# Merge of a hybrid diffusion block: branch sums for 1024 tokens at a time, then the output product as seven half-size products

## The chip, the cores and the metric

The kernel runs on one core of a Trainium2 chip. The metric is device time in microseconds (us), the median of the timed runs. The core has five engines with an instruction queue each: PE multiplies matrices into eight PSUM banks, DVE, ACT and POOL do elementwise work (POOL never reads PSUM), and SP issues nearly all transfers. All data is float32. For a product, each operand is split into a rounded part "hi" (type fp32r) and the remainder "lo", and three matmuls hi x hi, hi x lo, lo x hi are added up.

## The reference, cut to what matters

```python
# per token: attn_x (512), gm_x (512), ga_x, gb_x (1024 each); SEQ = 2048, D = 1024
y = sigmoid(ga_x) * (attn_x @ w_br_attn) + sigmoid(gb_x) * (gm_x @ w_br_gm)
x = x + g1 * (y @ w_out)
h2 = rmsnorm(x, norm2_g) * (1 + sc2) + sh2
x = x + g2 * (square(relu(h2 @ w_ff1)) @ w_ff2)      # D_FF = 4096
```

The whole layer also makes the modulation vectors, one combined input projection, the gMLP gating and grouped-query attention over 256 context and 2048 latent keys. They come before the part that changes.

## The kernel before, in words

The work is in four stages that PE goes through in order: projection, attention (`attend`), `merge`, and the feed-forward part (`ffn`). Tokens come in four blocks of 512 (`TB`), b = 0 to 3; spilled tensors in memory carry intermediate results between stages.

**Merge.** For each block b there are two steps. The branch step runs m = 0 to 7 over 128 output channels each: `fetch` loads the two 512x128 slices of the branch weights (`br_raw`, L853), splits them into hi and lo (`br_weights`, helper `split`: hi by ACT on L138, lo by POOL or DVE on L142) and loads two gate tiles (`gate_in`, L868), always two m ahead. 24 matmuls (L170 to L172, helper `mm3`) make two sums in PSUM; DVE multiplies each by its gate (L903), adds them (L906), and `split` makes the hi and lo of y. The outer step then multiplies y (eight tiles of 128 channels x 512 tokens) with `w_out`, which `load_w_out` has split once in block 0: four token tiles x two column halves x 24 matmuls. DVE multiplies by g1 (L941), adds x (L942), SP stores x1 (L944), and ACT sums the squares (L947) for the next norm. The inputs of the next block's branch step (`br_inputs`: attention and gMLP rows, softmax denominators, split into hi and lo, L832 to L842) are made beside the outer step.

**Feed-forward.** It works on two blocks of 1024 tokens, `blk` = 0 and 1, and computes each product of 2x2 half-size blocks with seven half-size products in place of eight (Strassen's scheme in Winograd's form). `h_ops` (L964 to L1010) reads x1, scales it by the norm (DVE, L981: one 128x2048 instruction for each of four kk), transposes it on PE (L176, 16 for each kk), applies scale and shift (ACT, L990), and makes the seven token operands with four DVE sums (L998 to L1007) and seven hi/lo pairs (`halves`: ACT on L961, DVE on L962). For block 0 this is called after the merge, with nothing beside it; for block 1 it is a side generator of the second product of block 0, `ff2`. `w1_ops` makes the weight operands of a group of 256 hidden channels (load L1017, DVE L1024 to L1046, ACT L1032 to L1045), one group ahead of its use. `ff1_group` (L1076 to L1078, helper `product`) does seven products of 12 matmuls. `w2_ops` prepares `w_ff2` in seven operands and stores them.

`ff2` has 7 x 8 steps of 24 matmuls, each on a chunk of two operands that `ff2_chunk` loads from memory (two transfers of 512 KB, L1162), rounds (ACT, L1163) and subtracts (DVE, L1164). A chunk takes four tiles of 4 KB per partition of the tag `f4`, which has 12 slots, so three chunks fit; the chunk of step n+2 is asked for in step n. The seven products go in the order 0, 1, 5, 6, 4, 2, 3. Products 0, 1, 5, 6, 3 add up in one set of four banks, 4 and 2 in another. After product 0, ACT copies the banks out (L1203); after 1, DVE makes a quarter of the output (L1176, two instructions a token tile) and ACT restores the banks from the copy (L1206); after 5 and 6 ACT copies again.

**Order.** A compile-time scheduler places the instructions of each queue by estimated times; `order` at the end adds constraints: tiles of one tag take their slots in program order, and SP's instructions inside `ff2` keep program order. At run time each queue is strictly in order. SBUF is given out in pools: `join` for the merge and `back` for the feed-forward part cannot be open together.

Of the kernel before, what the change touches and what calls it, by code (L numbers as in the profile page):

```python
# [9 lines left out]
F32 = mybir.dt.float32  # L10
# [8 lines left out]
P = 128  # L19
# [24 lines left out]
NCH = NG // 2  # L44


def f32(ap):
# [7 lines left out]
    "join": {"gt": 6, "bw": 14, "y": 16, "wo": 18, "xt": 3, "jk": 4},  # L55
    "back": {"h": 56, "f8": 3, "f4": 12, "f2": 16, "fs": 5},
# [7 lines left out]
class Kern:  # L64
# [50 lines left out]
    def small(self, shape, dtype=F32):  # L115
        return self.sb("fs" if "back" in self.open_pools else "ts", shape, dtype)
# [61 lines left out]
    def constants(self):  # L178
# [17 lines left out]
        self.ss2 = cp.tile([P, SEQ // P], F32, name="ss2")  # L196
# [16 lines left out]
        def operands(n):  # L213
            return [
                [
                    dp.tile([2, P, TB], F32, tag=f"{n}{p}_{c}", name=f"{n}_d{p}_{c}")
                    for c in range(NCH)
                ]
                for p in range(7)
            ]  # L220

        self.ao_d = [operands(f"ao{blk}") for blk in range(2)]
        self.wo_d = operands("w2o")
# [589 lines left out]
    def load_w_out(self):  # L813
        nc = self.nc
        self.wo = []
        self.g1b = self.sb("g1", [D])
        nc.sync.dma_start(self.g1b, self.g1_d.partition_broadcast(P)[:, 0, :])
        for k in range(KC):
            st = self.sb("wo", [D])
            nc.sync.dma_start(st, self.I["w_out"][0, k * P : (k + 1) * P, :])  # L820
            h, l = self.sb("wo", [D], F32R), self.sb("wo", [D], F32R)
            self.split(st, h, l, lo_eng="dve")
            self.wo.append((h, l))
            yield

    def br_inputs(self, b, out):
        nc = self.nc
        for nm, src in (("g", self.gm_d[b]), ("a", self.at_d[b])):
            out[nm] = []
            for k in range(4):  # L830
# [12 lines left out]
                h, l = self.sb("in", [TB], F32R), self.sb("in", [TB], F32R)  # L843
# [4 lines left out]
    def br_raw(self, m):  # L848
        out = {}
        for nm, key in (("a", "w_br_attn"), ("g", "w_br_gm")):  # L850
            out[nm] = self.sb("bw", [4, P])
            src = self.I[key][0][:, m * P : (m + 1) * P]
            self.nc.sync.dma_start(out[nm], src.rearrange("(k p) c -> p k c", p=P))  # L853
        return out

    def br_weights(self, raw, lo_eng="pool"):
        ws = {}
        for nm in ("g", "a"):
            wh, wl = self.sb("bw", [4, P], F32R), self.sb("bw", [4, P], F32R)
            self.split(raw[nm], wh, wl, lo_eng=lo_eng)  # L860
            ws[nm] = (wh, wl)
        return ws
# [8 lines left out]

    def merge(self, first, start, last):
        nc = self.nc
        for _ in start:
            pass
        self.close("mid", "base")
        self.open("join")
        steps = [(b, m) for b in range(NB) for m in range(KC)]
        it = iter(steps)
        q = []  # L880
        w_out = self.load_w_out()

        def fetch(lo_eng="pool"):
            s = next(it, None)
            if s is not None:
                q.append((self.br_weights(self.br_raw(s[1]), lo_eng), self.gate_in(*s)))

        inp = first
        early = [(s, self.br_raw(s[1])) for s in (next(it), next(it))]
        for s, raw in early:  # L890
            q.append((self.br_weights(raw, "dve"), self.gate_in(*s)))
        for b in range(NB):
            y = []
            for m in range(KC):
                fetch("pool" if b else "dve")
                ws, gt = q.pop(0)
                for nm in ("g", "a"):
                    ps = self.bank([TB])
                    wh, wl = ws[nm]
                    for k in range(4):  # L900
                        h, l = inp[nm][k]
# [674 lines left out]
```

## Time and profile before

| what | value |
|---|---|
| median of 3 timed runs | 3160.06 us (3157.05 to 3162.28) |
| profiled execution, first to last instruction (its span) | 3152.1 us |
| median less that span | 8.0 us |
| mean granted PE clock in that execution | 0.989 |
| merge in it, first branch matmul to last outer matmul | 1478.42 to 1847.40 us after the start |
| last matmul of the kernel issued | 3146.58 us |

The profile shows one execution, and gives no time for it besides its span. A row of the timeline gives the start, the duration, the engine, the line, the operation, the tiles (written <- read) and, in brackets, how long the engine had stood idle and what ended that. A matmul's duration is that of the pipeline; how fast PE works is read from the starts of neighbours. Rows of a stretch give the busy time of every engine (x instructions), the granted PE clock (1 is full) and the DMA engines' share and rate. "In", "bw", "gt", "y", "wo", "f", "h", "ac" are tags of tiles, "b" is PSUM.

### The profile page before, as it was taken

How to read it: one execution, taken by the hardware profiler on the slowest of the kernel's cores; microseconds unless marked ns; L12 is line 12 of the kernel's file. 1: busy time of each engine (PE TensorE's matmuls, PEld its weight loads, DVE VectorE, ACT ScalarE, POOL GpSimd, SP SyncE). 2: the span in 40 equal slices, each digit the busy share in tenths (PEclk: the TensorE clock that was granted, in tenths of full speed). 3: DMA queues.
4: the chain of work that ended last, by engine and by line, in shares of the span. 5: the costliest groups of instructions: out<-in, count | busy, mean ns of one | idle time of the engine just before them, and what ended most of it. 6: DMA issues, size and time to landing. Idle time of an engine off the chain costs nothing.

```text
span 3152.1 us, 38056 instructions
## 1 busy us (share of the span) xinstructions
PE 3057.4 (97%) x13892; PEld 2308.7 (73%) x13892; DVE 1944.7 (62%) x2797; ACT 1352.2 (43%) x2058; POOL 919.3 (29%) x634
## 2 busy tenths in 40 slices
PE   7999999999999999999999969999999999999999
PEld 4888788877655555555877858888777888888777
DVE  4735666566666677767644369777664576654445
ACT  3353434333454545454322135444543344443433
POOL 1423324241688888887134300000000000000000
PEclk9999999999999999999999989999999999999999
DMA  6353555535100000003754347988575644445665
GB/s 200 111 180 117 199 158 172 190 108 166 41 14 4 21 8 18 11 8 121 242 179 161 117 137 275 312 307 291 196 251 204 224 144 148 158 152 191 209 214 200
DMA packets 332174, 485.42 MB, mean 154 GB/s; under 512 B 33969, under 2 KB 166321, under 8 KB 331986
## 3 DMA queue, kind: packets, MB, share of 16 engines
q1 hardware_dynamic: 324002, 478.38, 45.4%
q10 hardware_dynamic: 7984, 4.61, 0.5%
q8 instruction: 109, 1.79, 0.2%
q14 instruction: 79, 0.65, 0.1%
HBM read 348.56 MB, written 134.35 MB: 153 GB/s over the span
## 4 chain that ended last, share of the span: by engine, by line
PE 78%; DVE 8%; DMA 5%; POOL 3%; issue 2%; ACT 2%; SPq 0%; ACTq 0%; DVEq 0%; POOLq 0%
PE b L1077 12%; PE b L1078 12%; PE b L1076 11%; PE b L1468 8%; PE b L170 7%; PE b L171 7%; PE b L172 7%; PE b L1435 5%; PE b L1454 4%; PE b L1400 3%; PE b L176 2%; DMA f<-w2o_d 1%; DMA w<-in_w_in 1%; DVE f L1164 1%; DMA bw<-in_w_br_gm 1%
## 5 line engine op out<-in xcount | busy, mean ns | idle before, releaser
L1164 DVE TENSOR_TENSOR f<-f,f 128x1024 fp32r<-128x1024 f32 x224 | 273.2, 1224 | 266.3 <-ACT f L1163 260.8
L1411 DVE TENSOR_REDUCE ts<-b 128x1 f32<-128x512 f32 x512 | 314.8, 683 | 175.7 <-PE b L1400 175.7
L1163 ACT CAST f<-f 128x1024 fp32r<-128x1024 f32 x224 | 235.3, 1053 | 332.4 <-DMA f<-ao_d 291.5
L1078 PE MATMUL b<-h,f 128*128 128x512 f32 x896 | 349.4, 390 | 9.1 <-DVE f L1033 7.2
L1077 PE MATMUL b<-f,f 128*128 128x512 f32 x896 | 351.5, 392 | 4.7 <-DVE f L1164 4.0
L1076 PE MATMUL b<-h,f 128*128 128x512 f32 x896 | 349.5, 391 | 3.4 <-ACT f L1032 3.4
L1078 PE MATMUL b<-f,f 128*128 128x512 f32 x896 | 349.4, 390 | 0.0
L1077 PE MATMUL b<-h,f 128*128 128x512 f32 x896 | 349.4, 390 | 0.0
L1076 PE MATMUL b<-f,f 128*128 128x512 f32 x896 | 307.5, 392 | 12.3 <-ACT f L1163 5.5
L1484 POOL TENSOR_TENSOR ac<-ac,p 128x512 f32<-128x512 f32 x216 | 296.3, 1403 | 71.4 <-ACT p L1458 70.5
L1458 ACT ACTIVATE p<-b 128x512 f32<-128x512 f32 x384 | 199.6, 616 | 157.5 <-PE b L1454 147.6
L142 POOL TENSOR_TENSOR w<-w,w 128x1024 fp32r<-128x1024 f32 x60 | 147.3, 2455 | 402.6 <-ACT w L138 204.1
L1484 POOL TENSOR_TENSOR ac<-ac,t 128x512 f32<-128x512 f32 x160 | 232.1, 1475 | 1.4 <-ACT t L1458 1.4
L138 ACT CAST w<-w 128x1024 fp32r<-128x1024 f32 x120 | 125.8, 1049 | 218.7 <-DMA w<-in_w_in 185.7
L170 PE MATMUL b<-t,w 128*128 128x512 f32 x512 | 204.8, 400 | 5.6 <-DVE t L584 5.2
L1076 PEld LDWEIGHTS b<-f,f 128*128 128x128 f32 x896 | 167.7, 188 | 53.6 <-ACT f L1163 9.6
L1077 PEld LDWEIGHTS b<-f,f 128*128 128x128 f32 x896 | 168.6, 188 | 46.0 <-DVE f L1164 11.6
L1078 PEld LDWEIGHTS b<-h,f 128*128 128x128 f32 x896 | 168.6, 188 | 45.7 <-DVE f L1033 7.9
L171 PE MATMUL b<-t,w 128*128 128x512 f32 x512 | 201.3, 393 | 0.0
L172 PE MATMUL b<-t,w 128*128 128x512 f32 x512 | 201.1, 393 | 0.0
L1435 PE MATMUL b<-t,t 128*128 128x512 f32 x576 | 198.7, 415 | 1.8 <-ACT p L1458 1.6
L1076 PEld LDWEIGHTS b<-h,f 128*128 128x128 f32 x896 | 168.9, 188 | 39.1 <-ACT f L1032 3.8
(217 smaller groups left out, 6137.9 us busy)
## 6 DMA issues: line engine op xcount, KB each, us to landing
w<-in_w_in SPq DMA_DIRECT2D x120, 512.0 KB
ao_d<-f SPq DMA_DIRECT2D x224, 256.0 KB
f<-ao_d SPq DMA_DIRECT2D x112, 512.0 KB
f<-w2o_d SPq DMA_DIRECT2D x112, 512.0 KB
f<-in_w_ff SPq DMA_DIRECT2D x48, 1024.0 KB
w2o_d<-f SPq DMA_DIRECT2D x112, 256.0 KB
md<-in_w_mod SPq DMA_DIRECT2D x32, 512.0 KB
f<-x_d SPq DMA_DIRECT2D x64, 256.0 KB
```

The costliest lines, as they stand in the source:

```text
L170: mm(ps, sh, mh, start=start, stop=False)
L171: mm(ps, sh, ml, start=False, stop=False)
L172: mm(ps, sl, mh, start=False, stop=stop)
L1076: mm(ps, wh, hh, start=start and k == 0, stop=False, skip_group_check=True)
L1077: mm(ps, wh, hl, start=False, stop=False, skip_group_check=True)
L1078: mm(ps, wl, hh, start=False, stop=k == len(w) - 1, skip_group_check=True)
L1163: nc.scalar.copy(h, f32(l))
L1164: nc.vector.tensor_tensor(out=l, in0=f32(l), in1=f32(h), op=ALU.subtract)
L1411: nc.vector.tensor_reduce(out=self.mx[:, t, h, c : c + 1], in_=ps[h], axis=AX.X, op=ALU.max)
L1435: self.nc.tensor.matmul(self.pts[j][h], k.KA[c][self.kv][:, ks], self.qa[h], start=True, stop=False, skip_group_check=True,)
L1468: nc.tensor.matmul(self.o[h * HD : (h + 1) * HD, :], k.V[c][:, i, self.kv * HD : (self.kv + 1) * HD], pt[h], start=j == 0, stop=j == NKT - 1,)
L1484: nc.gpsimd.tensor_tensor(out=self.acc[e][:, h], in0=old[:, h], in1=pt[h], op=ALU.add)
```

## The change

- The merge goes through pairs of blocks. `branches` (new) does the branch step of a block. For the first block of a pair, y is kept in SBUF (tag `y`) and stored as operands 0 and 1; for the second, every two m DVE makes the sums of Winograd's form from the four y tiles (four instructions of 128x512) and SP stores operands 3, 4, 5, 6 and 2. y is no longer split into hi and lo there.
- `w_out` is scaled by g1 (one DVE instruction of 128x2048 for each of four steps), combined with four DVE sums and stored in seven operands by `row_ops` (the renamed body of `w2_ops`), beside the branch step of block 0: a 1 MB load and seven stores of 256 KB for each step, two yields of it for each m.
- `rows` (the renamed body of `ff2`) does the output product as well: `out_rows(blk, side)` calls it with two chunks for each of seven products, so 14 steps of 24 matmuls for 1024 tokens. It loads x (four transfers of 256 KB for each of four quarters), DVE adds it, ACT sums squares into `ss2`, now for each column half, and writes the junk over the source.
- `h_ops(0)` becomes the side generator of `out_rows(1)` with two yields per step. For block 0 its 128x2048 scaling and its four sums go to POOL.
- `br_inputs` of the next block is made beside the branch step, in a second tag `in2` where needed.
- The weights of both branches of an m now share a tile of tag `f4`: three such tiles for an m (raw, hi, lo), one ACT and one POOL instruction of 128x1024. The `flow` tags, `f4` among them, are opened before the merge.
- In `rows`, so in `ff2` too, the order of the products is 0, 1, 5, 6, 3, 4, 2, and the result is written over the residual tile; in `ff2` the product with g2 is written over its source, which for products 1 and 3 is PSUM.

The core of the diff:

```diff
-    "join": {"gt": 6, "bw": 14, "y": 16, "wo": 18, "xt": 3, "jk": 4},
-    "back": {"h": 56, "f8": 3, "f4": 12, "f2": 16, "fs": 5},
+    "flow": {"f8": 3, "f4": 12, "f2": 16, "fs": 5},
+    "join": {"in2": 16, "gt": 6, "y": 8},
+    "back": {"h": 56},
...
+    def br_weights(self, m, lo_eng):
+        raw = self.sb("f4", [2, 4, P])
+        for i, key in enumerate(("w_br_gm", "w_br_attn")):
             src = self.I[key][0][:, m * P : (m + 1) * P]
+            self.nc.sync.dma_start(raw[:, i], src.rearrange("(k p) c -> p k c", p=P))
+        h, l = self.sb("f4", [2, 4, P], F32R), self.sb("f4", [2, 4, P], F32R)
+        self.split(raw, h, l, lo_eng=lo_eng)
+        return h, l
...
+    def branches(self, b, inp, fetch, y0, blk_ops, sides):
...
+        for m in range(KC):
+            fetch()
+            (wh, wl), gt = self.bq.pop(0)
...
+            y = self.sb("f2" if i else "y", [TB])
+            tt(y, gt["a"], gt["g"], add)
+            if i == 0:
+                y0[m] = y
+                nc.sync.dma_start(dst[f], y)
+            else:
+                y1[f] = y
+                if f:
...
+                    for p, src in ((3, a22), (4, s1), (5, s2), (6, s3), (2, s4)):
+                        nc.sync.dma_start(dst[p], src)
+            for it in sides:
+                next(it, None)
...
+            sides = [more]
+            if b == 0:
+                sides = [closing(), more, w_out, w_out]
+            elif b == 1:
+                sides = [w_out, w_out, more]
+            self.branches(b, inp, fetch, y0, self.yo_d[b // 2], sides)
...
+            if b == 1:
+                self.ready = [self.chunk(self.yo_d[0], self.wy_d, 0, 0)]
+                self.out_rows(0, iter(()))
         self.close("join", "pre")
         self.open("back")
+        self.ready = [self.chunk(self.yo_d[1], self.wy_d, 0, 0)]
+        h = [[None] * (KC // 2) for _ in range(7)]
+        self.out_rows(1, self.h_ops(0, h))
+        return h
...
+        def finish(i, j, t, src, x):
+            cs = slice(j * TB, (j + 1) * TB)
+            nc.vector.tensor_tensor(out=x, in0=src, in1=x, op=ALU.add)
+            col = (2 * blk + i) * TT + t
+            nc.scalar.activation(src, x, AF.Square, accum_out=self.ss2[:, j, col : col + 1])
+            return self.x1_d[2 * blk + i][t * P : (t + 1) * P, cs]
+
+        self.rows(self.yo_d[blk], self.wy_d, MCH, source, finish, side, 2)
...
+        eng = nc.vector if blk else nc.gpsimd
...
-            nc.vector.tensor_tensor(out=xv, in0=xv, in1=rb, op=ALU.mult)
+            eng.tensor_tensor(out=xv, in0=xv, in1=rb, op=ALU.mult)
...
-        order = (0, 1, 5, 6, 4, 2, 3)
-        steps = [(p, c) for p in order for c in range(NCH)]
+        order = (0, 1, 5, 6, 3, 4, 2)
+        steps = [(p, c) for p in order for c in range(chunks)]
         banks = {}
         for n, (p, c) in enumerate(steps):
             if n + 2 < len(steps):
-                ready.append(self.ff2_chunk(blk, *steps[n + 2]))
+                ready.append(self.chunk(ao, wo, *steps[n + 2]))
```

More of the change, by code (lines that the diff above doesn't have):

```diff
@@ L811, in attend, with br_inputs @@
         self.fixed.append(range(begin, self.here()))
[L813 to L826, printed above, removed]
+    def br_inputs(self, b, out, tag="in"):
         nc = self.nc
```

264 lines of the change are left out of this document (127 added, 137 removed).

## The prediction

> **What bounds the kernel now.** First the page's head and its slices, to see which engine sets the pace and where it doesn't.
>
> ```profile
> span 3152.1 us, 38056 instructions
> PE   7999999999999999999999969999999999999999
> ```
>
> PE is busy nearly always; each slice is 78.8 us, and the one weak slice, the 24th, is the hand-over from the merge to the feed-forward part. So a change pays in PE instructions saved, in PE's waits, and in that slice. Second, stretches of the merge: branch and outer steps of block 0, of block 1, the outer steps of blocks 2 and 3, the hand-over.
>
> ```profile
> core 0: us, PE busy (x) PEld busy (x) DVE busy (x) ACT busy (x) POOL busy (x), PEclk, DMA share, GB/s
> 1478.00:1526.00 48.00, 47.58 (x195) 37.16 (x196) 33.71 (x47) 21.24 (x34) 9.20 (x6) 0.96 0.83 271
> 1526.00:1570.00 44.00, 43.93 (x195) 36.00 (x193) 24.15 (x33) 12.34 (x20) 5.92 (x4) 1.00 0.72 238
> 1570.00:1615.00 45.00, 45.00 (x194) 36.25 (x193) 17.68 (x23) 11.49 (x20) 24.31 (x18) 1.00 0.48 148
> 1615.00:1664.00 49.00, 46.26 (x194) 36.97 (x193) 21.57 (x29) 11.58 (x20) 8.16 (x6) 0.97 0.55 186
> 1709.00:1759.00 50.00, 45.72 (x191) 36.42 (x190) 21.70 (x29) 11.52 (x20) 8.23 (x6) 0.97 0.48 164
> 1804.00:1848.00 44.00, 43.79 (x194) 35.90 (x192) 11.04 (x17) 4.07 (x7) 1.29 (x1) 1.00 0.13 48
> 1848.00:1894.00 46.00, 18.26 (x78) 14.94 (x79) 41.02 (x77) 27.56 (x45) 0.00 (x0) 0.67 0.64 189
> ```
>
> A step takes about 45 us whatever DVE, ACT and POOL do: PE bounds it. Only block 0's branch step is also near another limit, with DMA at 0.83. Third, the timeline of PE at the end of the merge.
>
> ```profile
> 1834.71 0.39 PE L170 MATMUL b<-wo,y 128*128 128x512 f32 x1
> 1835.39 0.39 PE L170 MATMUL b<-wo,y 128*128 128x512 f32 x1
> 1859.24 6.48 PE L176 MATMUL b<-ident,f 128*128 128x128 f32 x32 [11.45 <-DVE f L981]
> 1871.60 3.61 PE L176 MATMUL b<-ident,f 128*128 128x128 f32 x16 [3.40 <-ACT f L990]
> 1878.63 0.79 PE L1076 MATMUL b<-h,f 128*128 128x512 f32 x1 [3.43 <-ACT f L1032]
> 1887.07 0.80 PE L1078 MATMUL b<-h,f 128*128 128x512 f32 x1 [7.22 <-DVE f L1033]
> 1893.62 0.50 PE L1078 MATMUL b<-h,f 128*128 128x512 f32 x1 [1.92 <-DVE f L1040]
> ```
>
> The duration of 0.39 is not what a matmul costs: the two L170 rows are three matmuls and 0.68 us apart, 0.227 us each. A step of 24 is 5.44 us.
>
> **Fewer matmuls: -21.8 us.** The outer steps have 768; seven products x 2 chunks x 24 x 2 are 672. 96 x 0.227 = 21.8.
>
> **The waits inside the merge: -12.9 us.** The four outer steps take 44 + 49 + 50 + 44 = 187 us by their rows, 768 x 0.227 = 174.1. The difference is the wait for the hi and lo of the last y, which goes with its split:
>
> ```profile
> PE b L170 <- ACT y L138: 3.5, 3, 1.5
> PE b L172 <- POOL y L142: 3.5, 4, 1.0
> ```
>
> The rest of it is half clock after such waits (0.97 in two rows).
>
> **The hand-over: -36.1 us, of which 2 come back.** From 1848 to 1894 there are 46 us with 13 useful matmuls (2.9 us). The 64 transposes remain; at full clock 16 of them take 1.76 us (the chain of waits, in order of time), 7.0 in all:
>
> ```profile
> 2240.89 1.76 PE b L176 x16
> ```
>
> 46 - 2.9 - 7.0 = 36.1. Of these, 7.22 + 3.43 + 1.92 = 12.6 us belong to `w1_ops(0)`, which the change doesn't name. At the end of `ff2(0)` the same preparation is hidden, since the scheduler may issue it ahead; I take 2 us for it, between 0 and 12.6.
>
> **Block 0's transfers: +18 us, blocks 1 to 3: +4.** Sizes are in the DMA view:
>
> ```profile
> bw<-in_w_br_gm SPq DMA_DIRECT2D x32, 256.0 KB
> w2o_d<-f SPq DMA_DIRECT2D x112, 256.0 KB
> ```
>
> In units of 256 KB (0.262 MB), block 0's branch step now moves 16 of weights, 16 of gates, 12 of `br_inputs(1)`, 16 of `w_out`, 28 operand stores of `w_out` and 8 of y: 96 units, 25.2 MB, against 48 us x 271 GB/s = 13.0 MB. The densest long stretch is
>
> ```profile
> 1940.00:2000.00 60.00, 60.00 (x266) 49.70 (x265) 47.46 (x64) 27.24 (x40) 0.00 (x0) 1.00 0.91 318
> ```
>
> 318 / 0.91 = 349 GB/s at full share: 72 us, where PE needs 45. All of it goes through SP's one queue, so the weights for m+2 stand behind stores that wait for DVE. The last stores (2.1 MB, 6 us) aren't needed by PE: 66 us against 48. If the compile order puts the stores off into block 1 the term could be 0; with DVE's stores blocking SP it could be 27. Block 1 has 64 units, 48 us plus the 6 left over, of which the last 12 don't hold PE up: 47 for 45. Blocks 2 and 3 have 52 units each, 39 us under 45: +1 each (0 to 5). DVE in block 0 gets 16 sums and four scalings more (about 20 us by the durations quoted further down) on 34; that stays under 66.
>
> **out_rows(0): +19 us.** A chunk from its issue to the last subtraction, in `ff2`:
>
> ```profile
> 3130.45 0.36 SPq L1162 DMA_DIRECT2D f<-ao_d  x1
> 3130.91 0.42 SPq L1162 DMA_DIRECT2D f<-w2o_d  x1
> 3131.38 1.90 SPq L1185 DMA_DIRECT2D f<-x_d  x4
> ```
>
> ```profile
> 3136.65 1.23 DVE L1164 TENSOR_TENSOR f<-f,f 128x1024 fp32r<-128x1024 f32 x1 [0.27 <-ACT f L1163]
> ```
>
> That is 7.4 us. `ff2` hides it with three chunks in 12 slots of `f4`. Here `fetch` has already put the weights of block 2, m = 0 and 1, into four slots, and nothing frees them until the product is over. Two chunks fit: step n+2's load is issued when step n ends and must be ready when step n+1 ends. A step then takes (7.4 + 5.44) / 2 = 6.4 us; 12 x 1.0 = 12. Behind that waiting load on SP stand the four loads of x. For product 1 they come after its last step; x lands behind the chunk (about 5.5 us), then DVE adds, ACT squares and restores the bank for product 5 (0.7 + 2 x 0.6): 5.5 us more than the ordinary wait, and 1.7 of half clock. 12 + 7 = 19; 0 if the slots come free in time, 35 if the load is slower (second rival).
>
> **out_rows(1): +14 us.** PE needs 14 x 5.44 + 7.0 = 83.2 us. POOL's work beside DVE's:
>
> ```profile
> 1462.11 13.39 DVE L1481 TENSOR_TENSOR ac<-ac,p 128x1024 f32<-128x1024 f32 x6
> ```
>
> ```profile
> 1467.74 8.89 POOL L1484 TENSOR_TENSOR ac<-ac,t 128x512 f32<-128x512 f32 x4
> 1494.25 1.29 POOL L142 TENSOR_TENSOR y<-gt,y 128x512 fp32r<-128x512 f32 x1 [3.21 <-PE b L171]
> ```
>
> ```profile
> L1164 DVE TENSOR_TENSOR f<-f,f 128x1024 fp32r<-128x1024 f32 x224 | 273.2, 1224 | 266.3 <-ACT f L1163 260.8
> L142 POOL TENSOR_TENSOR w<-w,w 128x1024 fp32r<-128x1024 f32 x60 | 147.3, 2455 | 402.6 <-ACT w L138 204.1
> ```
>
> ```profile
> L962 DVE TENSOR_TENSOR h<-f,h 128x512 fp32r<-128x512 f32 x28 | 19.2, 685 | 0.0
> ```
>
> Alone a DVE instruction takes 1.22 and a POOL one 1.29; together each takes 2.22. They take turns, at 2.22 for 2.51. DVE instructions with both inputs in SBUF: 28 subtractions x 1.22, 28 halves and 8 sums of x x 0.685: 59 us. POOL: four scalings at twice 2.455 and 16 sums at 1.29: 40. 99 x 2.22 / 2.51 = 88 us; 16 sums that read PSUM (0.685 each), the norm's small instructions and the order within the queues make it about 97, 14 over PE. Transfers are 104 units, 78 us. Bounds: 0 (POOL's turns fall into gaps) to 30. The Trainium skill, "SBUF — State Buffer", section "Who interferes with whom", says that a DVE instruction with two SBUF inputs and a reading GpSimd instruction exclude each other for the whole instruction. By it the 88 are 99 and the term is 25; the measured pair decides.
>
> **ff2 and the start: +6.5 us.** The last product was 3 (two DVE instructions a tile) and is now 2 (three):
>
> ```profile
> 3143.61 0.69 DVE L1176 TENSOR_TENSOR f<-b,g2b 128x512 f32<-128x512 f32 x1 [5.73 <-PE b L1078]
> 3147.61 1.28 DVE L1176 TENSOR_TENSOR f<-f,f 128x512 f32<-128x512 f32 x2
> ```
>
> Eight end 5.28 us after the first starts, 0.66 each; twelve take 7.9, so the last store leaves 2.6 us later. After product 1 the restore waits for one DVE instruction more (the product with g2 is in PSUM now; a write there shows no price, I take the same 0.685):
>
> ```profile
> PE b L1076 <- ACT b L1206: 4.8, 4, 1.7
> ```
>
> ```profile
> 2247.00:2250.00 3.00, 3.00 (x9) 2.35 (x8) 2.60 (x5) 3.00 (x6) 0.00 (x0) 0.52 0.29 111
> 2295.00:2301.00 6.00, 3.59 (x14) 2.47 (x14) 6.00 (x9) 2.51 (x4) 0.00 (x0) 1.00 1.13 335
> ```
>
> ```profile
> 2245.62 0.50 PE L1076 MATMUL b<-f,f 128*128 128x512 f32 x1 [1.84 <-ACT f L1203]
> ```
>
> A wait of 1.84 us at 2245 was followed by 3 us at clock 0.52; the 1.7 us of L1206, in the stretch from 2295, left it at 1.00. With 0.7 more, those waits in each `ff2` may cross into that: 2 x 0.7 and one half clock in two, and product 3 now waits for the copies after 6: +2.4 (0 to 8). The Trainium skill, "TensorE: Matmul & The Clock Gate", section "What's actually happening", drops the clock only after an idle window of about 3.4 us; by it, waits under that are free of half clock and my sum is some 3 us lower, but the 1.84 us row speaks against it. At the start the weights of both branches must land before one cast of 1024 elements: +1.5 (0 to 6).
>
> **Sum.** -21.8 - 12.9 - 36.1 + 2 + 18 + 4 + 19 + 14 + 6.5 = -7.3 us against the profiled 3152.1, so 3144.8 there. The runs' median lies 8.0 above that span, and 8.0 is added again: 3152.8.
>
> **The rivals.**
>
> *All the cover holds (chance 0.2).* Stores slip into block 1, two chunks suffice, POOL falls into gaps: the terms +18, +19 and +14 shrink to 2, 5 and 3. -7.3 - 41 = -48: 3112. For it: in `ff1(0)` PE never waited at a DMA share of 0.91. Against: 25.2 MB can't go through in 45 us at 349 GB/s.
>
> *Slots of `f4` starve out_rows(0), slower than before (0.3).* A chunk load under dense traffic has taken
>
> ```profile
> 2305.71 10.87 DMA f<-w2o_d
> ```
>
> 10.9 us, and with cast and subtraction 13.1. A step is then (13.1 + 5.44) / 2 = 9.3, 12 steps cost 46 in place of 12: +34, in all +27: 3187. It decides from 6.44 + 7.3 / 12 = 7.0 us a step, a load of 8.7 us; from there the change loses. For it: 88 units in this stage, and product after product with loads of x and stores of x1. Against: the bare load is 7.4.
>
> *The operands are not made in time (0.05).* If POOL and DVE in turn finish `h_ops(0)` only after the last product, up to 15 us of the hand-over come back: 3168.
>
> **How the numbers follow.** The forecast, 3140 to 3165 around 3153, has 0.45. Within 0.2% is 6.3 us, about what a measurement of this kernel tells from no change. Faster by more: all of the first rival (0.2) and half of the forecast (0.23), 0.43. Within: 0.17 of the forecast and 0.05 of the slower cases, 0.22. Slower: the rest, 0.35. The range leaves a tenth out on each side: 3110, the first rival, to 3190, the second.
>
> **What would show it.** Right: 672 matmuls of the output product; no gap over 5 us between the merge and `ff1`; block 0's branch step at 60 us or more with DMA above 0.9; out_rows(0) at 6.4 us a step, PE waiting for the chunk's cast and once for the restore after product 1; out_rows(1) at 95 us or more with DVE instructions lengthened beside POOL; the end 2.6 us longer after the last matmul. Wrong: block 0's step under 55 us, or either product under 85 us (the first rival); a step over 7 us in out_rows(0) (the second).

## The result, and the profile after

The changed kernel takes 3276.74 us (median of four runs, 3273.64 to 3280.43) against 3158.56 for the kernel before in the same series (3153.25 to 3162.28): 1.0375 times as long, 95% interval 1.036 to 1.039. It was forecast at 3152.8, and it is 118 us slower. The profiled execution has a span of 3277.2 us, 125.1 more than before, at a mean granted clock of 0.975.

The stretches of the merge in the profile after, with the columns of the prediction's second fence: the branch steps of blocks 0 and 1; the time from there to the first step of out_rows(0); out_rows(0) with the branch steps of blocks 2 and 3 (the scheduler interleaves the end of one with the start of the next); out_rows(1).

```profile
1479.00:1623.00 144.00, 109.76 (x388) 80.10 (x388) 87.55 (x98) 23.64 (x28) 36.27 (x14) 0.87 0.86 275
1623.00:1645.00 22.00, 0.39 (x3) 0.16 (x1) 11.99 (x15) 6.66 (x9) 4.78 (x2) 0.56 0.78 252
1645.00:1848.00 203.00, 181.05 (x719) 140.08 (x720) 106.75 (x137) 66.31 (x97) 33.98 (x14) 0.94 0.70 228
1848.00:1980.00 132.00, 100.82 (x404) 76.57 (x403) 88.07 (x82) 70.20 (x113) 42.17 (x20) 0.88 0.66 218
```

Before, PE was busy in 0.91 to 1.00 of each step (the prediction's second fence). Here it is busy in 0.76 of blocks 0 and 1 and of out_rows(1), and in next to nothing of the 22 us ahead of out_rows(0). From the first branch matmul to the first matmul of `ff1` 500.9 us pass, against 400.2 before: 100.7 of the 125.1. What PE waited for in the first two stretches (engine, line, what ended the wait; total, times, longest):

```profile
PE b L172 <- ACT f L140: 22.2, 8, 5.4
PE b L1108 <- ACT f L1195: 21.6, 1, 21.6
PE b L174 <- POOL f L144: 14.4, 9, 2.0
```

L140 and L144 are the split of the branch weights: they came late. L1195 is the cast of the first chunk of out_rows(0). And in out_rows(1), where no wait leads:

```profile
PE b L1109 <- DVE f L1196: 9.8, 7, 4.7
PE b L1108 <- ACT f L1195: 9.5, 6, 5.4
PE b L178 <- POOL f L1005: 5.4, 1, 5.4
PE b L1108 <- ACT b L1241: 3.6, 1, 3.6
```

Waits cost more than themselves. At full clock the starts of neighbouring matmuls are at most 0.24 us apart; in the merge after, 182 matmuls follow at 0.30 to 0.45 us (half clock, after a wait), before 37. That alone is 31 us against 6.

The rest of the loss lies behind the merge: `ff1(0)` and `ff1(1)` are 1.9 and 10.5 us longer, though `ff1(0)` lost 8 us of waits and half clock, most at its start; `ff2(0)` is 7.9 longer, `ff2(1)` with the kernel's end 3.5. One row tells most of `ff1`, the same 270 us within `ff1(0)`, before and after:

```profile
1905.00:2175.00 270.00, 270.00 (x1192) 223.55 (x1192) 217.62 (x290) 128.58 (x186) 0.00 (x0) 1.00 0.88 309
```

```profile
2000.00:2270.00 270.00, 270.00 (x1154) 217.07 (x1153) 210.29 (x293) 124.85 (x181) 0.00 (x0) 1.00 0.84 294
```

PE never waits and the clock is full in both, and yet 1154 matmuls are done in place of 1192: 0.234 us each in place of 0.2265, for the same instructions. This time from one matmul's start to the next one's is called the cadence below.

### The profile page after: what moved, and what is told of

Its sections match the earlier page's. It is cut to its first block, busy times and chain, and to the rows that moved or that the text cites. A ratio compares the mean times of both kernels' runs of the same rounds, so it can differ in the third digit from the quotient of the medians.

```text
span 3277.2 us, 38226 instructions
## 1 busy us (share of the span) xinstructions
PE 3097.1 (95%) x13796; PEld 2308.8 (70%) x13796; DVE 2031.4 (62%) x2845; ACT 1400.9 (43%) x2106; POOL 932.2 (28%) x608
## 4 chain that ended last, share of the span: by engine, by line
PE 76%; DVE 9%; DMA 7%; ACT 3%; issue 2%; POOL 2%; SPq 1%; POOLq 0%; ACTq 0%; DVEq 0%
PE b L1109 13%; PE b L1110 13%; PE b L1108 12%; PE b L1499 7%; PE b L174 6%; PE b L172 6%; PE b L173 5%; PE b L1466 4%; PE b L1485 4%; PE b L1431 3%; PE b L178 2%; DVE f L1196 1%; DMA f<-in_x 1%; DMA f<-in_w_br_attn 1%; ACT f L1195 1%
## 5 line engine op out<-in xcount | busy, mean ns | idle before, releaser
L1196 DVE TENSOR_TENSOR f<-f,f 128x1024 fp32r<-128x1024 f32 x280 | 345.6, 1240 | 356.2 <-ACT f L1195 346.0
L1109 PE MATMUL b<-f,f 128*128 128x512 f32 x1120 | 450.2, 402 | 18.0 <-DVE f L1196 17.1
L1195 ACT CAST f<-f 128x1024 fp32r<-128x1024 f32 x280 | 293.3, 1051 | 404.2 <-DMA f<-ao_d 270.9
L1108 PE MATMUL b<-f,f 128*128 128x512 f32 x1120 | 396.6, 402 | 72.3 <-ACT f L1195 49.2
L1110 PE MATMUL b<-f,f 128*128 128x512 f32 x1120 | 445.3, 398 | 0.0
L1110 PE MATMUL b<-h,f 128*128 128x512 f32 x896 | 355.9, 397 | 2.3 <-DVE f L1058 2.1
L1108 PE MATMUL b<-h,f 128*128 128x512 f32 x896 | 355.6, 397 | 0.2 <-ACT f L1127 0.2
L1109 PE MATMUL b<-h,f 128*128 128x512 f32 x896 | 355.8, 397 | 0.0
L1108 PEld LDWEIGHTS b<-f,f 128*128 128x128 f32 x1120 | 214.0, 193 | 130.7 <-ACT f L1195 59.6
L1109 PEld LDWEIGHTS b<-f,f 128*128 128x128 f32 x1120 | 216.5, 193 | 77.1 <-DVE f L1196 32.4
L144 POOL TENSOR_TENSOR w<-w,w 128x1024 fp32r<-128x1024 f32 x60 | 147.7, 2462 | 401.5 <-ACT w L140 214.8
L1110 PEld LDWEIGHTS b<-f,f 128*128 128x128 f32 x1120 | 216.2, 193 | 44.8
L140 ACT CAST w<-w 128x1024 fp32r<-128x1024 f32 x120 | 125.8, 1048 | 222.6 <-DMA w<-in_w_in 201.5
L1110 PEld LDWEIGHTS b<-h,f 128*128 128x128 f32 x896 | 169.0, 189 | 44.5 <-DVE f L1058 2.6
```

The costliest lines, as they stand in the source:

```text
L1108: mm(ps, wh, hh, start=start and k == 0, stop=False, skip_group_check=True)
L1109: mm(ps, wh, hl, start=False, stop=False, skip_group_check=True)
L1110: mm(ps, wl, hh, start=False, stop=k == len(w) - 1, skip_group_check=True)
L1195: nc.scalar.copy(h, f32(l))
L1196: nc.vector.tensor_tensor(out=l, in0=f32(l), in1=f32(h), op=ALU.subtract)
```

## The experiments

Each is set against the kernel before on its own chip; times of the changed kernel's variants are to be read beside its 3276.7 us and ratio 1.0375. The diffs are cut to the lines that matter.

### What slows the matmuls of ff1

Starts of operands within a partition's memory are those of the compiled programs. My first idea was the start of the moving operand: slow where it is 96 mod 128 bytes. Three kernels move it with unused bytes.

```diff
     # e1: the kernel after
+    "flow": {"f8": 3, "f4": 12, "f2": 16, "fs": 5, "pf": 1},
+        self.nc.vector.memset(self.sb("pf", [16]), 0.0)
     # e2: the kernel before, pool of constants
+        self.pad = cp.tile([P, 16], F32, name="pad")
     # e3: the kernel before, the tile behind `in`
+        self.g1b = self.sb("g1", [D + 8])[:, :D]
```

> The kernel after, with one unused tile of 64 B per partition ahead of the join and back pools, so that every slot of the feed-forward operands h starts at 32 instead of 96 mod 128 bytes of a partition (in2, the branch inputs of blocks 1 and 3, likewise from 96 to 32; f4 from 64 to 0). Theory A, the start of the moving operand sets the matmul's cadence: the 2 x 1344 matmuls of the two first feed-forward products go from about 234 to 227 ns from start to start, some 20 us, and the 2 x 192 of branches 1 and 3 give up to 3 us more where they aren't waiting: 3276.7 falls to about 3255. Theory B, the slower cadence comes from what runs beside these products (transfers or the shared port) or from the clock: cadence and time stay, 3276.7 within 5 us.

> The kernel before with one unused tile of 64 B per partition in the pool of constants, so that h (moving in ff1) and f4 (moving in ff2, and stationary in ff1) start at 96 instead of 32 mod 128 bytes, and the stationary wo at 64 instead of 0. Theory A, the start of the moving operand sets the cadence: 4 x 1344 matmuls go from 227 to 234 ns, about 38 us slower, 3158.6 to about 3197 (ratio 1.012). Theory B, the cadence has to do with what runs beside the matmuls: no change, within 5 us.

> The kernel before with the branch inputs in moved by 32 B (the tile behind them is 32 B longer), so that they start at 64 instead of 96 mod 128 bytes. Theory A, the start of the moving operand sets the cadence: the 768 matmuls of the branches go from 233.3 to 226.8 ns, 5 us less, 3158.6 to about 3153.6 (ratio 0.9984). Theory B: no change.

Measured: e1 3272.4 us, ratio 1.0384 (1.0369 to 1.0398); e2 3158.4, 1.0016 (1.0007 to 1.0025); e3 3153.0, 0.9999 (0.999 to 1.0008). The cadence of `ff1` did not change: e1 still has 0.234, e2 0.2265.

```profile
2000.00:2270.00 270.00, 270.00 (x1154) 217.07 (x1153) 207.10 (x287) 120.82 (x175) 0.00 (x0) 1.00 0.85 296
```

```profile
1905.00:2175.00 270.00, 270.00 (x1193) 223.57 (x1192) 219.83 (x294) 130.97 (x190) 0.00 (x0) 1.00 0.87 305
```

Theory A fell, but these runs show what it missed: e1 and e2 had each moved `h` and `f4` together. What went with the cadence in all of them was the distance of the moving from the stationary operand. Next, equal offsets within 128 B:

```diff
     # e5: the kernel after; `in` moved by 32 B, `in2` and `h` by 96 B
+        self.g1b = self.sb("g1", [D + 8])[:, :D]
+        self.nc.vector.memset(self.sb("pj", [24]), 0.0)   # join
+        self.nc.vector.memset(self.sb("pb", [24]), 0.0)   # back
     # e6: the kernel before
+        self.g1b = self.sb("g1", [D + 24])[:, :D]
```

> The kernel after, with 96 unused bytes per partition ahead of the join and back pools and the branch inputs of blocks 0 and 2 moved by 32 B, so that in, in2 and h start at 64 mod 128 bytes, as f4 and f2, the stationary operands beside them, do (in after: 96, 96, 96 against 64). Theory C, the cadence is set by the two operands together: about 227 ns from start to start where moving and stationary operand start at the same offset within 128 B, 233 to 234 ns elsewhere. It gives 227 in both first feed-forward products, 2 x 1344 x 7.5 ns = 20 us, and up to 5 us in the branches where nothing else is waited for: 3272 to 3277 falls to 3248 to 3257 (ratio to the kernel before about 1.031). Theory B, the cadence comes from what runs beside these products: 234 stays, and the time within 5 us of after's.

> The kernel before with the branch inputs in moved by 96 B (the tile behind them is 96 B longer), so that they start at 0 mod 128 bytes as the stationary bw beside them does (before: 96 against 0; moved by 32 B, at 64 against 0, the cadence was still 233.3 ns). Theory C, equal offsets within 128 B give the short cadence: the 768 matmuls of the branches go from 233.3 to 226.8 ns, 5 us less, ratio about 0.9984. Theory B: no change of cadence or time.

e5: 3253.5 us, 1.0313 (1.0294 to 1.0332), by the ratios 20 us less, as theory C has it, and `ff1` has the short cadence again:

```profile
2000.00:2270.00 270.00, 269.89 (x1190) 222.79 (x1189) 213.01 (x293) 125.62 (x182) 0.00 (x0) 1.00 0.86 303
```

But e6 changed nothing, 0.9999 (0.999 to 1.0009): its branches stayed at 232 to 233 ns. In e5, too, blocks 0 and 2 stayed at 232, while blocks 1 and 3 went to 226.7. The compiled starts tell these apart within 256 B: in e5 `in2` and `h` lie 0 from `f4` there, `in` 128; in e6 `in` lies 128 from `bw`. So e11, the kernel before with `bw` moved to where `in` is:

```diff
+        self.nc.vector.memset(self.sb("pj", [56]), 0.0)   # 224 B, join
```

> The kernel before with 224 unused bytes per partition at the start of the join pool, so that bw starts at 224 mod 256 bytes as in does, and y and wo both at 224 (they were both at 0). Theory D, the short cadence comes where moving and stationary operand start at the same offset within 256 B (within 128 B was not enough in the branches of blocks 0 and 2: 232 ns): the branches' 768 matmuls go from 233.3 to 226.8 ns, 5 us less, 3152 to 3147, ratio 0.9984. Theory E, the branches' inputs are slow for another reason: cadence and time stay.

The branch step of block 2, before and in e11:

```profile
1671.00:1705.00 34.00, 34.00 (x148) 27.36 (x147) 13.43 (x19) 7.99 (x14) 19.17 (x14) 1.00 0.53 163
```

```profile
1671.00:1705.00 34.00, 34.00 (x152) 28.16 (x151) 15.51 (x19) 9.66 (x17) 17.70 (x14) 1.00 0.49 155
```

148 matmuls become 152; all four branch steps run at 226.7 ns. Theory D holds for the cadence. Its time does not follow: ratio 1.0000 (0.9991 to 1.0009). The merge takes 400.2 us as before, since most of what was won came back in the outer step's wait for hi of y:

```profile
PE b L170 <- ACT y L138: 7.6, 4, 2.8
```

It was 3.5 in the kernel before. There the 5 us of slower matmuls seem to have been cover for y's split.

### Blocks 0 and 1: order or bytes

39.6 MB in 144 us are 275 GB/s, at a DMA share of 0.86. e4 keeps SP's issues there in written order; e7 leaves 24 of the 28 stores of `w_out`'s operands out; e15 issues these stores from ACT's queue.

```diff
     # e4
+            begin = self.here()
             self.branches(b, inp, fetch, y0, self.yo_d[b // 2], sides)
+            if b < 2:
+                self.loads.append(range(begin, self.here()))
     # e7
+        for p, src in enumerate(srcs if scale is None else srcs[:1]):
     # e15
+            (nc.sync if scale is None else nc.scalar).dma_start(dst[p][s // 2][s % 2], src)
     # e4 and e15, ahead of the stores in row_ops
+        if scale is not None:
+            yield
```

> The kernel after, with SyncE's issues of blocks 0 and 1 kept in their written order (the fetch of weights two steps ahead stands in front of the step's stores) and the seven stores of w_out's operands written one step later, when their sums are old. The bytes are the same, and so is the work of VectorE. Theory A, SyncE's queue is what held block 0 and 1 back (the fetches of weights stand behind stores that wait for VectorE): the two blocks, 144 us, fall towards the 113 that the prediction gave them, 15 to 30 us less in the whole, about 3250. Theory B, the transfers' bytes hold them back: 144 within 4 us, and the time within 6 us of 3276.7. Theory C, VectorE's own load in these blocks holds them back, and the stores only showed it: 135 to 144.

> The kernel after without the stores of w_out's operands 2 to 7 (24 of its 28 stores, 6.3 MB); all seven products read operand 1 in their place, so the output product is another one, of the same size. The sums on VectorE are still made, and out_rows reads as many bytes as before. Theory B, the bytes through the DMA engines hold blocks 0 and 1: 39.6 MB in 144 us are 275 GB/s, so 6.3 MB less are about 23 us less, 144 to about 121, the whole about 3253. Theory C, VectorE's sums and the waits behind them hold the blocks: 144 within 5 us.

In the kernel after, the stores of `w_out`'s operands (L1101) waited in SP's queue for DVE, 19.6 us in eight waits:

```profile
SPq L1101 <- DVE f L1098: 10.6, 4, 3.8
SPq L1101 <- DVE f L1087: 9.0, 4, 4.2
```

e4: 3280.3 us, 1.0402 (1.0386 to 1.0418). Its stores wait for DVE for 1.6 us only, and yet the two blocks take 143.9 us, as before the edit: that wait was not what made them long. This looked like theory B. But e4 hadn't taken the burst away, as its timelines of SP and ACT show:

```profile
1505.93 6.06 SPq L1106 DMA_DIRECT2D wy_d<-f  x7
1512.04 0.45 SPq L1086 DMA_DIRECT2D f<-in_w_out  x1
1512.53 0.50 SPq L843 DMA_DIRECT2D f<-in_w_br_gm  x1
1513.08 0.67 SPq L843 DMA_DIRECT2D f<-in_w_br_attn  x1
```

```profile
1519.22 1.04 ACT L140 CAST f<-f 128x1024 fp32r<-128x1024 f32 x1 [10.22 <-DMA f<-in_w_br_attn]
```

Seven stores and the next megabyte of `w_out` are issued ahead of 512 KB of weights, which land 6 us after their issue; PE stands from 1514.7 to 1520.3. e7: 3257.3 us, 1.0328 (1.0305 to 1.035), 126.6 us for the blocks. That is 17 less, not the 23 that 6.3 MB are at 275 GB/s, and e7 had thinned out both bytes and burst. e15 parts the two.

> The kernel after with the 28 stores of w_out's operands issued from ScalarE's queue instead of SyncE's, one step later than in after. The bytes are the same; what no longer stands ahead of the branch weights in SyncE's queue are seven stores of 256 KB in a row. Theory A, the weights come late because they are queued behind these stores: blocks 0 and 1 fall from 144 to 115 to 130 us, the whole by 12 to 25. Theory B, the bytes through the DMA engines, whoever issues them: 144 within 5 us, the whole within 6 of 3276.7. If ScalarE, in order, then waits for VectorE's sums ahead of its casts, up to 10 us more.

e15: 3254.3 us, 1.0315 (1.03 to 1.0331); 125.5 us for the blocks, 18.4 less with not a byte less. Theory A.

```profile
1479.00:1600.00 121.00, 100.19 (x369) 74.01 (x370) 80.24 (x97) 23.45 (x28) 34.46 (x14) 0.90 0.94 315
```

This row is of the first 121 us. PE's wait for the cast of the weights fell from 22.2 to 8.4 us, and the DMA engines now work in 0.94 of the time, at 315 GB/s, so little is left to gain by order. SP's waits for DVE at the stores of y are about the same in e4 and e15 (23.4 and 25.6 us), so the difference between the two lies in the burst. Whether the order alone did it, or also that two queues issue side by side, was not parted.

### The 22 us ahead of out_rows(0), and its steps

SP's queue at the hand-over, in the kernel after (a few loads of gates and gMLP rows between these rows are left out):

```profile
1628.65 2.82 SPq L902 DMA_DIRECT2D yo_d<-f  x4
1631.56 0.98 SPq L902 DMA_DIRECT2D yo_d<-y  x1
1632.64 0.56 SPq L823 DMA_DIRECT2D raw<-at_d  x1
1633.29 1.20 SPq L827 DMA_DIRECT2D raw<-rs_d  x2
1634.58 0.54 SPq L1194 DMA_DIRECT2D f<-yo_d  x1
1636.74 0.37 SPq L1194 DMA_DIRECT2D f<-wy_d  x1
```

The last branch matmul starts at 1622.8; the first chunk's loads (L1194) leave 12 and 14 us later, behind stores and loads of blocks 1 and 2. e8a asks for this chunk in block 1 (its data are from block 0); e8b moreover fetches block 2's weights only behind out_rows(0).

```diff
     # e8a: a side generator of block 1
+        def early():
+            for _ in range(5):
+                yield
+            self.ready = [self.chunk(self.yo_d[0], self.wy_d, 0, 0)]
+            yield
...
     # e8b: the fetches of (2, 0) and (2, 1)
                 self.out_rows(0, iter(()))
+                for s in ((2, 0), (2, 1)):
+                    self.bq.append((self.br_weights(s[1], "dve"), self.gate_in(*s)))
```

> The kernel after with the first chunk of out_rows(0) fetched and split during block 1 (step 5 of 8) instead of behind it; the chunk's four slots of f4 are taken from the weights' fetches for that time. Theory A, the 22 us without a matmul between block 1 and out_rows(0) come from the chunk's load, which SyncE issues only behind the block's stores and loads: the gap falls to 2 to 5 us, and the whole by 13 to 19, to about 3260. Theory B, VectorE and the transfers are behind there anyway, and the second chunk is as late as the first: the gap moves to the next step, and the whole falls by less than 6.

> The kernel with the early first chunk (3266.5 us), and block 2's first two weights fetched behind out_rows(0) instead of ahead of it, so that all 12 slots of f4 serve the product's chunks (three chunks instead of two). Theory A, the slots of f4 hold out_rows(0) back (the second rival of the prediction): its steps go from about 7.5 to about 6 us, 15 to 20 us less over 14 steps, against 5 to 8 us more at block 2's start: 3250 to 3258. Theory B, the transfers and the order of the splits hold it back, not the slots: out_rows(0) within 5 us, block 2 later by 5 to 8, so 3268 to 3276.

e8a: 3266.5 us, 1.0353 (1.0335 to 1.0372); the gap falls from 22.0 to 5.0 us, but the second chunk is late by 7.4, and 10 us are left of the gain (7 by the ratios): between the theories. e8b: 3261.0, 1.0338 (1.0324 to 1.0353), also between its theories. From the last branch matmul of block 1 to that of block 3 pass 225.3 us in after, 214.6 in e8a and 210.2 in e8b. What the slots of `f4` do shows in the steps of out_rows(0), each from its first matmul to that of the next:

| kernel | steps 1 to 5 | steps 6 to 11 |
|---|---|---|
| after | 51.7 us: 9.8, 9.6, 8.6, 15.4, 8.2 | 41.3 us: 7.2, 6.2, 7.0, 5.9, 7.5, 7.4 |
| e8a | 56.6 us: 18.2, 10.0, 7.3, 13.8, 7.3 | 39.4 us: 7.2, 6.3, 6.7, 5.9, 7.3, 6.0 |
| e8b | 52.1 us: 10.9, 8.2, 7.6, 17.8, 7.7 | 32.6 us: 5.4 each |

With three chunks, steps 6 to 11 take no more than their 24 matmuls, so two chunks were what held these steps, 7 us in e8a. In after, SP's chunk loads waited for PE to free slots (all from 1645 to 1740 us):

```profile
SPq L1194 <- PE b L1110: 59.3, 10, 13.6
```

But steps 1 to 5 are as long with three chunks, so the slots are not their cause. In after, the two loads of a chunk are torn apart there by those of `br_inputs(2)` (L823, L827), which wait their turn for DVE:

```profile
1652.82 0.37 SPq L1194 DMA_DIRECT2D f<-yo_d  x1
1655.00 1.09 SPq L827 DMA_DIRECT2D raw<-rs_d  x2
1656.74 0.33 SPq L823 DMA_DIRECT2D raw<-at_d  x1
1657.11 0.43 SPq L1194 DMA_DIRECT2D f<-wy_d  x1
```

That this is what makes them late was not tried. Of the 7 us some 4 are left in e8b's sum, since PE waits longer there for the restored banks (11.7 us for 7.8) and for block 2's first weights (6.3 for 2.7).

In after, e8a and e8b there is a wait for the restored banks behind product 1. The timeline of after shows its order, from the last matmul of product 1 to the first of product 5:

```profile
1679.90 0.39 PE L1110 MATMUL b<-f,f 128*128 128x512 f32 x1
1680.10 0.36 SPq L1194 DMA_DIRECT2D f<-yo_d  x1
1681.02 2.02 SPq L1227 DMA_DIRECT2D f<-in_x  x4
1686.17 0.68 DVE L969 TENSOR_TENSOR f<-b,f 128x512 f32<-128x512 f32 x1
1687.64 0.59 ACT L1241 COPY b<-f 128x512 f32<-128x512 f32 x1
1688.28 0.79 PE L1108 MATMUL b<-f,f 128*128 128x512 f32 x1 [7.99 <-ACT b L1241]
```

The rows of x (L1227) are issued behind a chunk's loads that waited for a free slot. e12 loads them one step earlier:

```diff
-            if c == chunks - 1 and p in goes:
+            if c == max(0, chunks - pace) and p in goes:
```

> The kernel after with the residual rows of the output product loaded one step earlier in out_rows (at the first of a product's two chunks; the feed-forward's second product is as it was). Theory A, the 8.0 us behind product 1 in out_rows(0), and 3.6 in out_rows(1), come from this load, which SyncE issues only behind a chunk's load that waits for slots of f4: both waits fall to 2 to 3 us, the whole by 5 to 9, to about 3269. Theory B, the wait is the addition, square and copy themselves on VectorE and ScalarE: it stays above 6, and the time within 3 us.

In out_rows(0) the wait fell to 1.9 us in all, as theory A says:

```profile
PE b L1108 <- ACT b L1241: 1.9, 3, 1.2
```

The time did not move: 3276.5 us, 1.0391 (1.0375 to 1.0406). out_rows(1) took 145.2 us in place of 131.8, with 8.6 us at the same line. Its residual tiles now hold slots of `f2` longer, of which `h_ops` takes its sums; that this is the reason was only argued, and e14 below speaks against it as the whole reason.

### out_rows(1): the operands made beside it

```diff
     # e9
-        eng = nc.vector if blk else nc.gpsimd
+        eng = nc.vector
     # e10: SP's issues of w1_ops(0) and of the first ff1 group, held behind
+            self.loads.append(range(begin, self.here()))
     # e13
-        self.out_rows(1, self.h_ops(0, h))
+        self.out_rows(1, iter(()))
+        for _ in self.h_ops(0, h):
+            pass
```

> The kernel after with h_ops(0)'s scaling and sums on VectorE instead of GpSimd (as h_ops(1) has them). Theory A, the two engines take turns and GpSimd's 42 us beside out_rows(1) lengthen VectorE's remainders, so that chunks come late: out_rows(1), 131 us, falls by 8 to 15, the whole to 3262 to 3269. Theory B, VectorE then has 35 us more of its own on 88 in 131 us, and nothing falls: out_rows(1) within 4 us or longer by up to 15. Theory C, SyncE's blocked issues set out_rows(1) (23 us behind loads of w1 and w2): within 4 us either way.

> The kernel after with SyncE's issues of the first group of ff1 kept behind those of out_rows(1) (in after the loads of w1 and w2 stand between out_rows(1)'s chunks and wait there for a slot of f8, 14.6 and 8.5 us). Theory C, the blocked queue makes chunks late: out_rows(1) falls from 131 by 10 to 20 us, and ff1's first operands come up to 13 us later, since their load then starts at the product's end; the whole 3262 to 3275. Theory A, GpSimd beside VectorE sets out_rows(1): it falls by less than 5, and the whole rises to 3277 to 3290.

> The kernel after with h_ops(0) written behind out_rows(1) instead of beside it (the order in which engines do the operations may still let some of it run early). Theory A, the operands made beside the product cost it most of its 49 us over the 83 of its matmuls and transposes: out_rows(1) without them takes 92 to 102 us, and then 40 to 46 us follow in which TensorE waits for them, as in the kernel before: the whole 3277 to 3297. Theory B, out_rows(1) is late by its own chunks: it stays above 115, and the operands come on top: above 3305.

e9: 3263.1 us, 1.0346 (1.033 to 1.0362); out_rows(1) 122.4 us in place of 131.8, though DVE has POOL's work besides: theory A. Its busy time did not even rise (88.07 us in the row of after above):

```profile
1844.00:1967.00 123.00, 100.53 (x404) 77.62 (x403) 85.42 (x103) 70.20 (x113) 0.00 (x0) 0.88 0.71 236
```

e10: 3288.2 us, 1.0419 (1.0398 to 1.044). The product's matmuls end after 128.5 us, 3 earlier, and then PE waits for w1's operands:

```profile
PE b L1108 <- ACT f L1057: 12.5, 1, 12.5
```

The issues that stood blocked in SP's queue were not what made chunks late. e13: 3294.9 us, 1.0437 (1.0413 to 1.046). Nearly free of the operands, the product takes 98 us; 43 follow:

```profile
1857.00:1955.00 98.00, 87.03 (x370) 68.79 (x368) 54.28 (x54) 50.07 (x77) 9.07 (x4) 0.95 0.66 231
1955.00:1998.00 43.00, 7.81 (x35) 6.66 (x33) 34.91 (x47) 22.74 (x43) 25.80 (x15) 0.57 0.43 138
```

So the hidden hand-over is worth 43 us and its cover costs 34: theory A.

### Together

e14 puts e5 (at one offset within 256 B for all), e8b, e9 and e12 together; e16 adds e15.

> The kernel after with what helped put together: moving and stationary operands of all branches and of the first feed-forward products at the same offset within 256 B (224), the first chunk early, block 2's weights behind out_rows(0), h_ops(0) on VectorE, the residual rows a step earlier. If the parts add up: 3276.7 less 23 (the e5 kernel's, with blocks 0 and 2 too), 15.7, 13.6 and 7, so about 3217. If they share the same waits: 3225 to 3245. In both cases slower than the kernel before, since blocks 0 and 1 keep their bytes (144 us against 92 or 93).

> The kernel of e14 (3217.5 us) with the stores of w_out's operands issued from ScalarE's queue, one step later. If theory A of e15 holds: 3192 to 3206. If theory B holds: 3211 to 3224. In both cases slower than the kernel before.

e14: 3217.5 us, 1.0200 (1.0185 to 1.0216), where the forecast had it if the parts add up. That sum had 7 us for e12, which alone brought none; by the ratios the parts alone are 20, 12, 9 and 0 us, and together 55. The earlier load of e12 seems to pay here: out_rows(1) takes 122.0 us, as in e9, so e12's loss there is gone with the sums on DVE. e16: 3203.6, 1.0161 (1.0142 to 1.018), 14 less again. What is left in e16, in the stretches of the first fence:

```profile
1477.00:1604.00 127.00, 103.57 (x388) 77.81 (x388) 86.36 (x98) 23.48 (x29) 35.49 (x14) 0.91 0.94 308
1604.00:1612.00 8.00, 0.00 (x0) 0.00 (x0) 6.40 (x10) 2.17 (x3) 0.00 (x0) 0.72 0.58 202
1612.00:1805.00 193.00, 176.16 (x720) 138.45 (x720) 115.35 (x144) 69.55 (x102) 34.61 (x14) 0.96 0.79 261
1805.00:1928.00 123.00, 97.97 (x402) 74.59 (x401) 87.57 (x105) 72.12 (x115) 0.00 (x0) 0.90 0.74 246
```

That is 451 us for the 400 of the kernel before. No version of the change came under the kernel before.

## Why the prediction was wrong

The prediction's terms make 396.8 us from the first branch matmul to `ff1`; it took 500.9. With 22.8 in `ff1`, 6.4 in `ff2` and its end, and 0.9 less at the start, this is the whole miss, 132.4 us on the profiled span. (The median is off by 124: it lies 0.5 below the span in the kernel after, so the 8.0 us that the prediction added to the span were no constant.) What failed is the way of the sum: it added bytes over a rate and busy times of engines, and put too little, at the start of out_rows(0) nothing, for waits that come from the order within the queues.

| step of the prediction | as it put it | measured | what the runs showed in its place |
|---|---|---|---|
| blocks 0 and 1, transfers | 66 + 47 = 113 us | 74.7 + 69.1 = 143.9 | 18.4 of it stores in SP's queue (e15); the rest is the rate, 312 GB/s over e15's two blocks and not 349 |
| out_rows(0) starts at once | 0 | 22.0 | the first chunk's loads stand behind block 1's stores and block 2's loads (e8a) |
| out_rows(0), blocks 2 and 3 | 95 + 92 = 187 | 109.3 + 93.9 = 203.3 | steps 1 to 5 took 24 us over their matmuls, 12 forecast; the slots' price was near the forecast, 1.4 us a step in steps 6 to 11 for 1.0 (e8b) |
| out_rows(1) | 83 + 14 = 97 | 131.8 | 34 from the operands beside it (e13), 9.4 of them POOL's turn (e9); without them 98, not 83 |
| `ff1` as before | 0, and its waits at the start gone but for 2 | +22.8 beside that | 20 from the offset of `h` against `f4` (e5) |
| `ff2` and its end | 2.4 + 2.6 = 5.0 | 8.8 + 2.6 = 11.4 | the restore after product 1 waits 4.3 us in each, not 2.4; in `ff2(0)` PE waits 11.2 us for chunks, 4.9 before, and why was not tried |

**Blocks 0 and 1** failed first in a choice. The prediction saw "the weights for m+2 stand behind stores that wait for DVE", priced it at 27 at most, and took 18, worked out from the bytes at a rate that the busiest stretch of `ff1(0)` had shown. There, PE needs a megabyte of weights every 19 us (84 matmuls). Here it needs 512 KB every 5.4 us (24), and 2.9 MB issued in one burst ahead of them are 9 us at 315 GB/s, most of the two steps by which they are fetched ahead. What would have shown it was forecast as "DMA above 0.9": it was 0.84 in block 0, and 0.94 only in e15. The wait of these stores for DVE, which the prediction named, was not what mattered (e4); the burst in SP's queue was (e15). With the stores on ACT's queue block 0 takes 59.9 us, under its 66, and block 1 still 65.7 for 47, with the DMA engines 0.93 busy at 306 GB/s.

**The start of out_rows(0)** was not in the sum at all. The prediction followed the queue past the stores in block 0, but not at the end of block 1, where the first chunk comes last.

**out_rows(0)** was right in its mechanism, and short in size: PE waited for the chunk's cast, and once, 8.0 us, for the restore (7 forecast). The two-chunk pace, forecast at 6.4 us a step, is 6.9 in steps 6 to 11, and gone with three chunks. Over the first 11 steps the mean is 8.45 us, above the 7.0 that the prediction gave as the sign of its second rival; but the surplus lies in steps 1 to 5, which three chunks don't shorten. (Block 2 interleaves with the last steps; the table counts each distance between starts to the matmul that ends it.)

**out_rows(1)** was summed as busy times of DVE and POOL, 97 us. Their busy times stayed below that (88 and 42), and PE waited all the same: here a chunk's remainder (L1196) stands in DVE's queue behind three halves that POOL stretches, and PE waits 4.65 us for it.

```profile
1931.60 6.39 DVE L980 TENSOR_TENSOR h<-f,h 128x512 fp32r<-128x512 f32 x3
1937.91 1.21 DVE L1196 TENSOR_TENSOR f<-f,f 128x1024 fp32r<-128x1024 f32 x1
```

```profile
1939.18 0.79 PE L1109 MATMUL b<-f,f 128*128 128x512 f32 x1 [4.65 <-DVE f L1196]
```

```profile
1930.68 2.15 POOL L1032 TENSOR_TENSOR f<-f,f 128x512 f32<-128x512 f32 x1 [1.29 <-DVE h L980]
1932.79 4.05 POOL L1005 TENSOR_TENSOR f<-f,fs 128x2048 f32<-128x2048 f32 x1
```

Three halves are 2.06 us alone and took 6.39, 4.3 more, while POOL worked for 5.2 of them. The Trainium skill, "SBUF — State Buffer", section "Who interferes with whom", has such instructions exclude each other whole; in these rows the delay of 4.3 us is most of the 5.2. By the prediction's pair of rows (2.22 us for 2.51) it is somewhat less than whole.

**Right** were the 672 matmuls; the hand-over to `ff1`, hidden but for 2.5 us (2 forecast); blocks 2 and 3, whose transfers stayed hidden; the tail, 2.6 us longer as forecast, 8.1 for 5.5 behind the last matmul. In `ff2` the row of the restore is 4.3 us in each block, 2.4 before in two waits; why it grew by 1.9 and not by 0.7 was not tried:

```profile
PE b L1108 <- ACT b L1241: 4.3, 1, 4.3
```

The range's upper end, 3190, came from the second rival, one mechanism. Six terms were short at once, most by waits that come from order and not from work; the further waits also brought half clock, 25 us more of it in the merge, for which the sum had 1.7. That the cadence of `ff1` would change was in no term and no rival.

## What to carry to other kernels

Transfers issued in a burst on the queue that also fetches the next step's operands make these late, here by 5 us at a time: price the burst against the prefetch distance, not only the bytes against the stage, and try another queue for bulk stores. Work moved beside a product is paid in the order of the queues that feed that product; cover of 43 us cost 34 here although the engines had room. When buffers move, look at the cadence of matmuls that were not edited.

## What the runs showed of the hardware

**Two operands and the cadence of a matmul.** 128x128 by 128x512 fp32r matmuls, one behind another at full clock, follow at 226.7 to 226.9 ns where moving and stationary operand start at the same offset within 256 bytes of a partition, and at 232 to 234 ns at the five other offsets seen. Offsets are moving less stationary, mod 256, from the compiled programs:

| kernel, product | offset | ns |
|---|---|---|
| before, `ff1`; e2, `ff1`; both kernels, `ff2` | 0 | 226.7 to 226.9 |
| after, `ff1` and branches; e1, `ff1`; e2, branches | 160 | 234.3 |
| before, branches | 224 | 233.3 |
| e3, branches | 192 | 233.3 |
| e5, branches of blocks 0 and 2; e6, branches | 128 | 232 to 233 |
| e1, branches of blocks 0 and 2 | 96 | 233.5 |
| e5, `ff1` and branches of blocks 1 and 3; e11, branches; e14, `ff1` | 0 | 226.7 |

Why two operands should meet in this way was not tried. The offset within 512 bytes is not what counts: in e5 `h` lies 256 from `f4` there and is at 226.7.

**Rate of the DMA engines.** 24 fewer stores left them at 262 GB/s and a share of 0.81 in blocks 0 and 1; all 28 stores from a second queue brought 315 at 0.94. One queue is no limit in itself: the prediction's stretch of `ff1(0)` shows 318 GB/s at 0.91 with SP issuing. In blocks 0 and 1 the order in that one queue, or the time that its issues take, kept the engines below what they can do.
